# The second feed-forward product of a decoder layer by 26 products over 4 token, 4 feature and 2 column blocks, with input sums on GpSimd and products chained in PSUM

## The chip, the core and the metric

The kernel runs on one core of a Trainium2 chip. Time is the device time of one execution in microseconds; the number that counts is the median of the runs. The engines are named as in the profile: PE (TensorE, matmul), PEld (its weight loads), DVE (VectorE), ACT (ScalarE), POOL (GpSimd) and SP (SyncE, which issues most of the transfers).

## The reference

One layer for 2048 tokens of width 1024, in float32: a norm, a combined input projection, gated linear attention in four heads and dilated window attention in eight, an output projection, and then the part that the change touches:

```python
h = h + jnp.einsum('bsm,md->bsd', mixed, w_out[l])

nm = rmsnorm(h, mlp_norm_g[l])
a = jnp.square(jax.nn.relu(jnp.einsum('bsd,df->bsf', nm, w_ff1[l])))
h = h + jnp.einsum('bsf,fd->bsd', a, w_ff2[l])
return rmsnorm(h, final_norm_g)
```

`a` is 2048 x 4096, `w_ff2` is 4096 x 1024. `a` is called the activations below, and its product with `w_ff2` the second product.

## The kernel before

Every float32 operand of a matmul is split into a high part in `fp32r` (ScalarE, a copy that rounds) and a low part, the difference (VectorE; `split`, L346 and L347). `mm3` (L67 to L69) then makes three matmuls of each pair: high x high, low x high, high x low, all into one PSUM bank. The weights side of such a matmul is 128x128, the moving side 128x512.

Both feed-forward products are computed by a Strassen scheme over 2 x 2 x 2 blocks: seven block products in place of eight, in the order j = 1, 2, 5, 6, 3, 4, 7, with sums of blocks made ahead (inputs) and behind (outputs).

*First product.* Tokens stand in two halves. A group `g` is 256 features of one half; there are 16 groups in each, 32 in all, and a job is one of the seven products of a group, 12 matmuls. `prep1` splits the weights of the job that comes two later (with four sums on the weights, L1090 to L1095) and `product1` runs the job. Its results go through PSUM into four accumulators c11, c12, c21, c22 of 128x512, are squared after a ReLU (`square`, L1118 and L1119, on ScalarE), and become inputs of the second product's Strassen scheme: four sums of 128x512 on VectorE per group (L1144 to L1147), and seven stores into `actD` (L1122). GpSimd has nothing to do there. Between the halves the seven transformed inputs (`hb`) are loaded and split anew.

*Second product.* It runs over 14 phases, which are the seven products for each half. A phase has 8 steps of 2 blocks of 128 features and 4 tiles of 128 tokens, so 8 x 2 x 4 x 3 = 192 matmuls, into four PSUM banks. `prep_a` splits a step's activations (128x1024, `ca` from `ra`), `prep_b` the weights (`cb` from `rb`), with sums on VectorE (L1235) where the scheme wants them; `taken` adds a finished bank to the running sums of the output (L1276), and `output` applies the last norm, with a gain on GpSimd (L1252), and stores. The banks rotate over the four PSUM tags a, c, d and o, 8 banks in all.

A scheduler that simulates the engines sets the order of instructions on each engine from the order of the code; an engine then runs its instructions strictly in that order. Transfers are mostly issued on SP, also in order, so a transfer that waits for its data holds back those behind it. Large buffers are slots of one ring (`slot`, 25 of them), handed out in turn.

```python
def mm2(p, n, c, i):
    l, r = comb_a[n % 3], comb_b[n % 8]
    tk = slice(i * 128, i * 128 + 128)
    mm3(p, l[:, 0, c, tk], l[:, 1, c, tk], r[:, 0, c], r[:, 1, c], n % 8 == 0 and c == 0, n % 8 == 7 and c == 1)
```

Of the kernel before, what the change touches and what calls it, by code (L numbers as in the profile page):

```python
# [10 lines left out]
F32 = mybir.dt.float32  # L11
# [29 lines left out]

def emit(tc, a, stop=99):
# [23 lines left out]
    def mm3(out, sh, sl, mh, ml, first, last):  # L66
        T.matmul(out, sh, mh, start=first, stop=False)  # L67
        T.matmul(out, sl, mh, start=False, stop=False)  # L68
        T.matmul(out, sh, ml, start=False, stop=last)  # L69
# [10 lines left out]
    V.memset(mhalf, -0.5)  # L80
    stats = const.tile([128, 96], F32, name="stats")
# [61 lines left out]
    actD = dram.tile([7, 2, FF // 256, 128, 512], F32, name="actD")  # L143
    tD = dram.tile([2, FF // 256, 128, 512], F32, name="tD")
# [960 lines left out]
    def product1(at):  # L1105
        g, j = jobs1[at]
        half, gh = divmod(g, NP)
        if not acc1:
            acc = [slot("acc1") for _ in range(4)]
            acc1.extend(t[:, 512 * q:512 * q + 512] for t in acc for q in range(4))  # L1110
        X, c11, c12, c21, c22, s2, s4 = acc1[7 * (g % 2):7 * (g % 2) + 7]
# [9 lines left out]
        def store(q, n, v):  # L1121
            q.dma_start(actD[n - 1, half, gh], v)  # L1122

        if j in (1, 5, 4):
            A.activation({1: X, 5: c22, 4: c21}[j], p, AF.Copy)
        elif j == 2:
            V.tensor_tensor(c11, p, X, op=OP.add)
            square(c11)
            store(A, 1, c11)
# [3 lines left out]
        elif j == 3:  # L1133
            V.tensor_tensor(c12, p, c12, op=OP.add)
            square(c12)
        else:
            V.tensor_tensor(X, p, X, op=OP.add)
            V.tensor_tensor(c21, c21, X, op=OP.add)
            V.tensor_tensor(c22, c22, X, op=OP.add)
# [43 lines left out]
    w2 = a["w_ff2"].rearrange("o (c p) n -> p (o c) n", p=128)  # L1183
    out2 = a["out"].rearrange("o s d -> (o s) d")
    order2 = (1, 2, 5, 6, 3, 4, 7)
    phases = [(j, half) for j in order2 for half in range(2)]
    raw_a, comb_a, raw_b, comb_b, sums = [], [], [], [], {}

    def load_a(n):

        if n < 4 * len(phases):
            j, half = phases[n // 4]
            if len(raw_a) < 2:
                raw_a.append(view(slot("ra"), (4, 512)))
            SP.dma_start(raw_a[n % 2], actD[j - 1, half, 4 * (n % 4):4 * (n % 4) + 4].rearrange("c p s -> p c s"))

    def prep_a(n):

        if n >= 8 * len(phases):
            return
        if len(comb_a) < 3:
            comb_a.append(view(slot("ca", FR), (2, 2, 512)))
        c = comb_a[n % 3]
        split(c[:, 0], c[:, 1], raw_a[n // 2 % 2][:, n % 2 * 2:n % 2 * 2 + 2])
        if n % 2:
            load_a(n // 2 + 2)  # L1210

    def load_b(n):

        if n >= 56:
            return
        j, c = order2[n // 8], 2 * (n % 8)
        if len(raw_b) < 2:
            raw_b.append(view(slot("rb2"), (2, 2, 512)))
        pairs2 = tD.rearrange("k c p s -> k p c s")
        of = {(k, m): w2[:, 2 * c + k:2 * c + k + 3:2, 512 * m:512 * m + 512] for k in range(2) for m in range(2)}  # L1220
# [204 lines left out]
```

## Time and profile before

| what | us |
|---|---|
| median of 3 runs (2354.55 to 2360.78) | 2357.18 |
| span of the profiled execution | 2353.6 |
| TensorE busy in it | 2288.2 |
| VectorE busy | 1563.8 |
| ScalarE busy | 1148.4 |
| GpSimd busy | 516.7 |

The profiled execution's own total isn't listed apart from its span; the runs shown lie 1 to 7 us above that span. A group's row reads: line, engine, operation, output tile <- input tiles, shapes and count, then busy time in us and mean in ns, then the idle time of the engine just before these instructions and what ended it. A row of the timeline has start and duration in us first. A row of a stretch has its length, the busy time of PE, PEld, DVE, ACT and POOL with counts, the clock that TensorE was granted (1.00 is full), the share of the transfer engines and GB/s.

### The profile page before, as it was taken

To read this page: it belongs to the slowest core of one execution; us is meant where nothing else is said; L and a number is where in the kernel's file an instruction comes from. 1 tells how busy PE (TensorE), PEld (TensorE's weight loads), DVE (VectorE), ACT (ScalarE), POOL (GpSimd) and SP (SyncE) were. 2 spreads that over 40 slices of the span, in tenths; PEclk is the share of its full clock that TensorE was granted. 3 is DMA by queue.
4 is the path that set the end of the run, shared out by engine and by line. 5 is a ranking of instruction groups with operands and counts; after the bars stand their busy time and mean duration, and the time that the engine had idled before them with its cause. 6 is when DMAs were issued, how large, how long until landed. Compare 5 with 4: busy or idle time off the path is not lost.

```text
span 2353.6 us, 34983 instructions
## 1 busy us (share of the span) xinstructions
PE 2288.2 (97%) x12648; PEld 1976.9 (84%) x12648; DVE 1563.8 (66%) x2873; ACT 1148.4 (49%) x2202; POOL 516.7 (22%) x578
## 2 busy tenths in 40 slices
PE   5999999999999997999999999999999999999998
PEld 5977899789999996888888888888888888888886
DVE  6888767766667676345877779777764356446545
ACT  5575536534677673223655557555554223224323
POOL 4343224236468768000000000000000100001002
PEclk9999999999999998999999999999999999999999
DMA  6458743857577755567844447444476486457643
GB/s 158 122 161 251 236 155 110 263 168 249 182 228 238 251 183 185 183 215 254 263 154 148 148 148 273 148 152 154 158 264 236 169 284 239 146 178 249 212 165 108
DMA packets 340939, 458.11 MB, mean 195 GB/s; under 512 B 18020, under 2 KB 214133, under 8 KB 334494
## 3 DMA queue, kind: packets, MB, share of 16 engines
q1 hardware_dynamic: 336014, 447.23, 58.4%
q10 hardware_dynamic: 4752, 8.65, 1.0%
q8 instruction: 99, 1.62, 0.3%
q14 instruction: 74, 0.61, 0.1%
HBM read 293.51 MB, written 167.02 MB: 196 GB/s over the span
## 4 chain that ended last, share of the span: by engine, by line
PE 85%; DMA 5%; DVE 4%; issue 2%; POOL 2%; ACT 2%; SPq 0%; POOLq 0%; DVEq 0%; ACTq 0%
PE ps_a L68 9%; PE ps_a L69 9%; PE ps_a L67 9%; PE ps_c L69 7%; PE ps_c L68 7%; PE ps_c L67 7%; PE ps_d L67 4%; PE ps_d L69 4%; PE ps_d L68 4%; PE ps_a L684 4%; PE ps_o L67 3%; PE ps_o L68 3%; PE ps_o L69 3%; PE ps_d L665 2%; PE ps_c L643 2%
## 5 line engine op out<-in xcount | busy, mean ns | idle before, releaser
L1252 POOL TENSOR_TENSOR suma<-suma,gs 128x512 f32<-128x512 f32 x16 | 23.3, 1470 | 1142.2 <-ACT scr L1250 1142.1
L347 DVE TENSOR_TENSOR ca<-ra,ca 128x1024 fp32r<-128x1024 f32 x112 | 137.8, 1231 | 165.6 <-ACT ca L346 165.6
L346 ACT ACTIVATE ca<-ra 128x1024 fp32r<-128x1024 f32 x112 | 117.9, 1053 | 222.2 <-PE ps_c L69 183.5
L346 ACT ACTIVATE w1comb<-w1raw 128x512 fp32r<-128x512 f32 x224 | 140.1, 627 | 157.2 <-PE ps_c L69 58.9
L347 DVE TENSOR_TENSOR w1comb<-w1raw,w1comb 128x512 fp32r<-128x512 f32 x224 | 154.2, 691 | 55.1 <-ACT w1comb L346 55.1
L656 ACT ACTIVATE pe<-pe,O 128x256 f32<-128x256 f32 (+1 forms) x384 | 155.6, 454 | 52.0 <-DVE O L655 50.3
L684 PE MATMUL ps_a<-v,pt 128*128 128x65 f32 x1200 | 178.0, 251 | 2.3 <-ACT pt L672 2.0
L684 PEld LDWEIGHTS ps_a<-v,pt 128*128 128x128 f32 x1200 | 174.5, 193 | 4.3 <-ACT pt L672 2.4
L665 PE MATMUL ps_d<-ident,pe 128*128 128x128 f32 x600 | 158.6, 278 | 1.1 <-ACT pe L656 1.1
L655 DVE CUSTOM_DVE_ANT_0 pe<-ps_c,nb 128x256 f32<-128x256 f32 (+1 forms) x384 | 126.4, 361 | 37.8 <-PE ps_d L665 15.6
L202 ACT ACTIVATE wcomb<-wraw 128x512 fp32r<-128x512 f32 (+2 forms) x126 | 96.9, 773 | 86.9 <-POOL wraw L208 14.6
L346 ACT ACTIVATE cb<-rb 128x1024 fp32r<-128x1024 f32 x56 | 59.4, 1061 | 162.8 <-PE ps_o L68 111.4
L69 PE MATMUL ps_c<-hb,w1comb 128*128 128x512 f32 x336 | 130.9, 389 | 0.0
L67 PE MATMUL ps_c<-cb,ca 128*128 128x512 f32 x336 | 130.8, 389 | 0.0
L68 PE MATMUL ps_c<-cb,ca 128*128 128x512 f32 x336 | 130.8, 389 | 0.0
L68 PE MATMUL ps_c<-hb,w1comb 128*128 128x512 f32 x336 | 130.8, 389 | 0.0
L69 PE MATMUL ps_c<-cb,ca 128*128 128x512 f32 x336 | 130.8, 389 | 0.0
L67 PE MATMUL ps_c<-hb,w1comb 128*128 128x512 f32 x336 | 130.8, 389 | 0.0
L204 DVE TENSOR_TENSOR wcomb<-wraw,wcomb 128x512 fp32r<-128x512 f32 (+2 forms) x84 | 99.3, 1188 | 36.7 <-ACT wcomb L202 36.4
L665 PEld LDWEIGHTS ps_d<-ident,pe 128*128 128x128 f32 x600 | 108.3, 185 | 1.8 <-ACT pe L656 1.5
L347 DVE TENSOR_TENSOR cb<-rb,cb 128x1024 fp32r<-128x1024 f32 x56 | 68.3, 1222 | 61.9 <-ACT cb L346 61.9
L67 PE MATMUL ps_a<-wcomb,tb 128*128 128x256 f32 (+1 forms) x336 | 97.9, 292 | 9.3 <-ACT tb L346 3.7
(359 smaller groups left out, 7206.3 us busy)
## 6 DMA issues: line engine op xcount, KB each, us to landing
ra<-actD SPq DMA_DIRECT2D x56, 1024.0 KB, 6.3
actD<-acc SPq DMA_DIRECT2D x192, 256.0 KB, 2.5
rb<-w_ff SPq DMA_DIRECT2D x72, 512.0 KB, 4.6
w1raw<-w_ff SPq DMA_DIRECT2D x32, 1024.0 KB, 5.5
k<-kD SPq DMA_DIRECT2D x16, 1024.0 KB, 9.3
rb<-hTD SPq DMA_DIRECT2D x13, 1024.0 KB, 5.7
wraw<-w_in SPq DMA_DIRECT2D x48, 256.0 KB, 3.3
cmb<-boD SPq DMA_DIRECT2D x16, 528.0 KB, 6.0
```

Source lines behind the costliest of these rows:

```text
L67: T.matmul(out, sh, mh, start=first, stop=False)
L68: T.matmul(out, sl, mh, start=False, stop=False)
L69: T.matmul(out, sh, ml, start=False, stop=last)
L202: A.activation(hi, src, AF.Copy, scale=sc)
L204: V.tensor_tensor(lo, src, hi.bitcast(F32), op=OP.subtract)
L346: A.activation(hi, src, AF.Copy)
L347: V.tensor_tensor(lo, src, hi.bitcast(F32), op=OP.subtract)
L643: T.matmul(s, q, k_cols(k1, br, first), start=True, stop=False)
L655: V.tensor_tensor_reduce(p, s, bias, scale=1.0, scalar=BIG, op0=OP.add, op1=OP.min, accum_out=nm)
L656: A.activation(p, p, AF.Exp, bias=nm, scale=-1.0)
L665: T.transpose(pb[:, i * 128:i * 128 + 128], src, ident)
L684: T.matmul(self.b.opsum[:, n % 4], self.pt[:, i * 128:i * 128 + 128], self.b.v[:, blk, cols], start=first, stop=last)
```

## The change

The second product is made over 4 token blocks, 4 feature blocks and 2 column blocks at a time: 26 block products in place of the 32 of a plain product (the Strassen scheme before makes 28 of them). A table `PRODUCTS` says for each product which stored activation row it takes, whether it starts a new PSUM bank or goes on in the one of the product before it, its sign, and which outputs the bank is then added to; `WEIGHTS` says which weight blocks are loaded and summed, `SUMS` how the 26 activation rows come out of the 16 blocks of a pair of groups.

- In `product1` the four VectorE sums and the stores go. The four accumulators of a group now stand in one slot of four, and the intermediate X in two other places.
- `token_sums` makes, for each pair of groups, 28 sums of 128x256 on GpSimd, two or three behind each job of the next pair, and stores 26 rows of 128x256 (four of them are blocks without a sum).
- The second product has 52 phases (26 products x 2 halves) of 8 steps, each step one block of 128 features x 2 tiles of 128 tokens x 3 matmuls, into two banks. `prep_s` splits activations (two pieces of 128x1024 a phase), `prep_t` weights (four pieces of 128x1024 a weight, six buffers), `add_t` sums weights on GpSimd (128x1024), all at steps that are fixed ahead of their use.
- `taken` adds a bank to one to four outputs in the two steps after its phase. `output` squares each half row when it is finished.
- The ring has 26 slots.

```diff
-        return up.tile([128, SLOT], dt, name=name, tag="u", bufs=25)[:, :n]
+        return up.tile([128, SLOT], dt, name=name, tag="u", bufs=26)[:, :n]
...
-            square(c22)
-            square(c21)
-            store(SP, 4, c22)
-            store(SP, 2, c21)
-            V.tensor_tensor(X, c12, c22, op=OP.add)
-            V.tensor_tensor(s2, X, c11, op=OP.subtract)
-            V.tensor_tensor(c12, c11, c12, op=OP.subtract)
-            V.tensor_tensor(s4, c21, s2, op=OP.subtract)
-            for n, v in ((5, X), (6, s2), (7, c12), (3, s4)):
-                store(SP, n, v)
+            square(c21)
+            square(c22)
...
+        for l, r in SINGLES:
+            store(r, t[l])
+        yield
+        for l, x, op, y, r in SUMS:
+            G.tensor_tensor(t[l], t[x], t[y], op=OP.add if op == "+" else OP.subtract)
+            if r is not None:
+                store(r, t[l])
+            yield
...
+        for cs, x in parts:
+            A.activation(v[:, 0, cs], x, AF.Copy, scale=float(sign))
+            if sign == 1:
+                V.tensor_tensor(v[:, 1, cs], x, v[:, 0, cs].bitcast(F32), op=OP.subtract)
+            else:
+                V.scalar_tensor_tensor(v[:, 1, cs], x, -1.0, v[:, 0, cs].bitcast(F32), op0=OP.mult, op1=OP.subtract)
+        load_s(ph + 2, u)
...
+            G.tensor_tensor(d, x, y, op=OP.add if op == "+" else OP.subtract)
+            if stored:
+                SP.dma_start(tD[:, 2 * u:2 * u + 2], d)
...
+        for l, sign in PRODUCTS[k][3]:
+            m, n = divmod(l, 2)
+            c = sums[half, m][:, i, 512 * n:512 * n + 512]
+            V.tensor_tensor(c, c, p, op=OP.add if sign > 0 else OP.subtract)
+            if last_at[l] == k:
+                output(half, l, i)
...
+        mm3(p, l[:, 0, c % 4, tk], l[:, 1, c % 4, tk], r[:, 0, c % 2], r[:, 1, c % 2],
+            PRODUCTS[ph // 2][1] == 1 and c == 0, c == 7, PRODUCTS[ph // 2][1] == 0)
...
+    for ph in range(2 * NR):
+        for u, n in ((0, -7), (1, -3)):
+            at_step(4 if (ph, u) == (1, 1) else 8 * ph + n, prep_s, ph, u)
...
+        for u in range(4):
+            at_step(at + (-16, -12, -9, -6)[u], add_t, q, u)
+        for u in range(4):
+            at_step(at + ((-12, -8, -5, -2) if q else (-10, -8, -5, -2))[u], prep_t, q, u)
```

In the order of VectorE, the end of one group and the start of the next in the first product, before (`w1comb` is the split weights, `w1raw` the raw ones, `acc` the accumulators, `ps_` a PSUM bank):

```order
L1137 TENSOR_TENSOR acc_11516<-ps_d,acc_11516 128x512
L1093 TENSOR_TENSOR w1raw<-w1raw 128x4x128
L1138 TENSOR_TENSOR acc_11517<-acc_11517,acc_11516 128x512
L1139 TENSOR_TENSOR acc_11517<-acc_11517,acc_11516 128x512
L347 TENSOR_TENSOR w1comb<-w1raw,w1comb 128x512
L1095 TENSOR_TENSOR w1raw<-w1raw 128x4x128
L347 TENSOR_TENSOR w1comb<-w1raw,w1comb 128x512
L1127 TENSOR_TENSOR acc_11515<-ps_o,acc_11515 128x512
L1144 TENSOR_TENSOR acc_11516<-acc_11517 128x512
L347 TENSOR_TENSOR w1comb<-w1raw,w1comb 128x512
L1145 TENSOR_TENSOR acc_11518<-acc_11516,acc_11517 128x512
L1146 TENSOR_TENSOR acc_11517<-acc_11517 128x512
```

The same place after the change, where L1192 is the old L1127, the first drain of a group (`gs` and `xt` hold X):

```order
L1201 TENSOR_TENSOR xt<-ps_d,xt 128x512
L1161 TENSOR_TENSOR w1raw<-w1raw 128x4x128
L1202 TENSOR_TENSOR acc_11517<-acc_11517,xt 128x512
L1203 TENSOR_TENSOR acc_11517<-acc_11517,xt 128x512
L415 TENSOR_TENSOR w1comb<-w1raw,w1comb 128x512
L1163 TENSOR_TENSOR w1raw<-w1raw 128x4x128
L415 TENSOR_TENSOR w1comb<-w1raw,w1comb 128x512
L1192 TENSOR_TENSOR acc_11518<-ps_a,gs 128x512
L415 TENSOR_TENSOR w1comb<-w1raw,w1comb 128x512 x2
L1195 TENSOR_TENSOR gs<-ps_c,gs 128x512
L415 TENSOR_TENSOR w1comb<-w1raw,w1comb 128x512
L1196 TENSOR_TENSOR acc_11518<-gs,acc_11518 128x512
```

The sums L1144 to L1147 have gone from between the splits, and what is left stands in the order that it had.

On GpSimd, before, the last sums of the attention stand directly ahead of the small powers of the norms and the gains of the second product (L1252); nothing of the first product is between them:

```order
L742 TENSOR_TENSOR cmb<-cmb,small 128x4x128 x2
L744 TENSOR_TENSOR O_9490<-O_9490,cmb 128x4x128 x2
L94 TENSOR_TENSOR stats<-stats,mhalf 128x1 x16
L1252 TENSOR_TENSOR suma<-suma,gs 128x512 x5
L94 TENSOR_TENSOR stats<-stats,mhalf 128x1 x2
```

After the change the same place begins the sums of the first pair of groups (`xt` also holds the three extra tiles that sums are made in):

```order
L812 TENSOR_TENSOR O_9491<-O_9491,cmb 128x4x128 x2
L162 TENSOR_TENSOR stats<-stats,mhalf 128x1 x16
L1224 TENSOR_TENSOR xt<-acc_11517 128x256
L1224 TENSOR_TENSOR acc_11517<-acc_11517 128x256 x2
L1224 TENSOR_TENSOR xt<-acc_11517,acc_11518 128x256
L1224 TENSOR_TENSOR acc_11517<-acc_11518 128x256
L1224 TENSOR_TENSOR acc_11518<-acc_11518 128x256
```

These run in their fixed order through the 16 pairs, 448 in all, before the first weight sum (L1320) of the second product.

In the second product VectorE's order has, after the change, the additions of a bank (L1364) between the low parts of activations (L1298 and L1300, `cs` from `rs`) and of weights (`ct` from `rt`):

```order
L1364 TENSOR_TENSOR acc_11518<-acc_11518,ps_c 128x512
L1364 TENSOR_TENSOR acc_11518<-acc_11518,ps_o 128x512
L1298 TENSOR_TENSOR cs<-rs,cs 128x1024
L415 TENSOR_TENSOR ct<-rt,ct 128x1024 x2
L1298 TENSOR_TENSOR cs<-rs,cs 128x1024
L1364 TENSOR_TENSOR sum<-sum,ps_a 128x512
L1364 TENSOR_TENSOR sum<-sum,ps_c 128x512
L1300 SCALAR_TENSOR_TENSOR cs<-rs,cs 128x1024
```

Before, the sums of weights (L1235) stood among the low parts, and the additions came for four banks together:

```order
L347 TENSOR_TENSOR cb<-rb_15946,cb 128x1024
L347 TENSOR_TENSOR cb<-rb_15942,cb 128x1024
L347 TENSOR_TENSOR ca<-ra,ca 128x1024
L1235 TENSOR_TENSOR rb_15946<-rb_15946 128x1024
L1276 TENSOR_TENSOR sumb<-sumb,ps_a 128x512
L1276 TENSOR_TENSOR sumb<-sumb,ps_d 128x512
L1276 TENSOR_TENSOR sumb<-sumb,ps_c 128x512
L1235 TENSOR_TENSOR rb_15942<-rb_15942 128x1024
```

The weight sums have moved to GpSimd, and the additions to places between low parts, two banks at a time.

More of the change, by code (lines that the diff above doesn't have):

```diff
@@ L1108, in product1 @@
         if not acc1:
[L1109 to L1111 removed]
+            acc1.extend(slot("acc1") for _ in range(4))
+        X = gM[:, :512] if g % 2 else xt[:, :512]
+        c11, c12, c21, c22 = [acc1[g % 4][:, 512 * n:512 * n + 512] for n in range(4)]
         p = bank()
@@ L1181, in emit @@
         late = (h, u[:, 0], t)
-    w2 = a["w_ff2"].rearrange("o (c p) n -> p (o c) n", p=128)
+    w2 = a["w_ff2"].rearrange("o (c q p) n -> q p (o c) n", q=4, p=128)
     out2 = a["out"].rearrange("o s d -> (o s) d")
[L1185 to L1199, printed above, removed]
@@ L1308, in emit @@
+    for k, (m, at) in enumerate(first_at.items()):
+        for half in range(2):
+            at_step(16 * at + 8 * half - 1 if at else 2 * half * k + k - 7 + 7 * half, load_c, half, m)
+    for ph in range(2):
+        for u in range(2):
+            at_step(4 * ph + u - 20, load_s, ph, u)
     rb.append(slot("rb"))
@@ L1330, in emit @@
         product1(at)
+        for _ in range(2 if at % 14 else 3):
+            next(ts, None)
+        if at % 14 == 13:
+            ts = token_sums(at // 7)
         for n in parts_at.get(at, ()):
```

270 lines of the change are left out of this document (146 added, 124 removed), and 31 rows, old and new, of tables (SUMS, WEIGHTS).

## The prediction

> **What bounds the kernel now.** The page first (engines, then the chain), then the stretches of the span, and last the groups of the two feed-forward products.
>
> ```profile
> span 2353.6 us, 34983 instructions
> PE 2288.2 (97%) x12648; PEld 1976.9 (84%) x12648; DVE 1563.8 (66%) x2873; ACT 1148.4 (49%) x2202; POOL 516.7 (22%) x578
> PE 85%; DMA 5%; DVE 4%; issue 2%; POOL 2%; ACT 2%; SPq 0%; POOLq 0%; DVEq 0%; ACTq 0%
> ...
> 900.00:1000.00 100.00, 88.50 (x454) 74.04 (x453) 49.39 (x77) 24.59 (x56) 36.34 (x58) 0.93 0.48 156
> ...
> 1160.00:1400.00 240.00, 240.00 (x1061) 198.86 (x1060) 180.67 (x280) 134.17 (x230) 0.00 (x0) 1.00 0.44 150
> 1400.00:1460.00 60.00, 59.53 (x263) 48.98 (x262) 54.36 (x77) 43.18 (x68) 0.00 (x0) 1.00 0.73 257
> 1460.00:1730.00 270.00, 270.00 (x1193) 223.72 (x1192) 205.50 (x318) 154.15 (x261) 0.00 (x0) 1.00 0.47 161
> 1740.00:2340.00 600.00, 599.60 (x2646) 496.42 (x2645) 306.07 (x329) 197.02 (x241) 28.74 (x26) 1.00 0.59 204
> ```
>
> The columns of a stretch are its length, busy time of PE, PEld, DVE, ACT and POOL, then clock, DMA share and GB/s. From 1160 us on TensorE has no gap and its clock is full: in the first product (to about 1737 us) it loses 0.47 us, where the second half's inputs are reloaded, and in the second product 0.40 us. Only fewer matmuls help here, and nothing else is late yet. 599.6 us / 2646 = **0.2267 us a matmul**; the means of 389 and 390 ns below overlap and aren't the pitch.
>
> ```profile
> L67 PE MATMUL ps_c<-cb,ca 128*128 128x512 f32 x336 | 130.8, 389 | 0.0
> L69 PE MATMUL ps_o<-cb,ca 128*128 128x512 f32 x112 | 43.6, 390 | 0.0
> ```
>
> These are the first and last of twelve such groups (four PSUM tags, three lines): 1008 + 672 + 672 + 336 = 2688 matmuls, as 14 phases x 8 x 2 x 4 x 3 say.
>
> **Term 1, the matmuls.** 26 products x 2 halves x 8 blocks x 2 token tiles x 3 = 2496 of the same form and order (128x128 against 128x512, three into one bank). 192 fewer x 0.2267 = **-43.5 us**, all on the path.
>
> **Term 2, the end.** After the last matmul the old code makes two sums and two squares before the norm; the new one makes one of each, since the other half row was squared before.
>
> ```profile
> 2344.85 0.69 DVE L1276 TENSOR_TENSOR suma<-suma,ps_o 128x512 f32<-128x512 f32 x1
> 2346.05 0.61 ACT L1250 ACTIVATE scr<-suma 128x512 f32<-128x512 f32 x1
> 2346.89 0.63 ACT L1250 ACTIVATE scr<-sumd 128x512 f32<-128x512 f32 x1
> ```
>
> The one square can start at about 2345.6 instead of 2346.89: **-1.3 us**. Its cover, the earlier sum and square of the other half row, is products away.
>
> **Term 3, the first product.** Per group of 256 features the four sums on VectorE (L1144 to L1147) go, 8 per pair of groups; GpSimd gets 28 sums of 128x256 per pair. A pair is 168 matmuls x 0.2267 = 38.1 us. Rows for one sum:
>
> ```profile
> L813 POOL TENSOR_TENSOR gla<-gla 128x256 f32<-128x256 f32 x16 | 11.7, 730 | 0.2
> L261 POOL TENSOR_TENSOR acc<-acc,misc 128x248 f32<-128x248 f32 x16 | 17.5, 1098 | 22.8 <-DVE acc L260 16.4 <-issue 6.4
> 100.00:200.00 100.00, 95.09 (x520) 78.10 (x521) 86.50 (x151) 67.74 (x153) 36.42 (x34) 1.00 0.53 161
> actD<-acc SPq DMA_DIRECT2D x192, 256.0 KB, 2.5
> ```
>
> Alone it takes 0.73 us; a slightly smaller one took 1.10 in stretches like this one, with VectorE 86.5% busy. Two of the 28 overwrite a tile whose store has just been issued (the second sum after the first, the seventh after the fifth); with 2.5 us a store I put 5 us for both. GpSimd then needs 28 x 0.73 + 5 = 25.4 to 28 x 1.10 + 5 = 35.8 us of 38.1: it fits, and four accumulators let it run into the next pair.
>
> What it costs VectorE is a port:
>
> ```profile
> 230.24 0.68 DVE L304 TENSOR_TENSOR acc<-ps_c,acc 128x512 f32<-128x512 f32 x1
> 230.47 1.29 POOL L214 TENSOR_TENSOR wraw<-wraw 128x512 f32<-128x512 f32 x1 [1.90 <-DVE wcomb L206]
> 230.84 1.47 DVE L206 SCALAR_TENSOR_TENSOR wcomb<-wraw,wcomb 128x512 fp32r<-128x512 f32 x1
> ...
> 297.89 1.22 DVE L204 TENSOR_TENSOR wcomb<-wraw,wcomb 128x1024 fp32r<-128x1024 f32 x1
> 299.03 1.22 DVE L347 TENSOR_TENSOR tb<-xp,tb 128x1024 fp32r<-128x1024 f32 x1
> ...
> 298.51 4.01 POOL L208 TENSOR_TENSOR wraw<-wraw 128x1024 f32<-128x1024 f32 x1 [18.85 <-DMA wraw<-w_in]
> 319.02 2.40 POOL L212 TENSOR_TENSOR wraw<-wraw 128x1024 f32<-128x1024 f32 x1
> ```
>
> L206, with both inputs in SBUF, takes 1.47 us and ends 0.55 after the GpSimd sum does; L304, with one input in PSUM, is not touched. The other way round the GpSimd sum at 298.51 takes 4.01 us where one of its size takes 2.40: two VectorE instructions, started every 1.14 us, kept it out. So they exclude each other, and VectorE's trains win. The Trainium skill states this exclusion (SBUF — State Buffer, § Who interferes with whom): whichever issues second blocks fully. By that rule, with the port held for whole instructions, the sum would be the second rival's 2341 and not 2317; the trace agrees that they exclude, but the 0.55 us behind the release shows less than the whole 0.69 held.
>
> ```profile
> 1457.73 0.68 DVE L1138 TENSOR_TENSOR acc<-acc 128x512 f32<-128x512 f32 x1
> 1458.33 0.68 DVE L1139 TENSOR_TENSOR acc<-acc,acc 128x512 f32<-128x512 f32 x1
> L347 DVE TENSOR_TENSOR w1comb<-w1raw,w1comb 128x512 fp32r<-128x512 f32 x224 | 154.2, 691 | 55.1 <-ACT w1comb L346 55.1
> ```
>
> Back to back a 128x512 costs VectorE 0.60 us (1457.73 to 1458.33), not 0.69. Left per pair are 36 (28 with two SBUF inputs, 8 from PSUM): 36 x 0.60 = 21.6 us; if each of the 28 waited for a whole sum (0.60 of it after overlap) 38.4 us, just the pair's 38.1. Operands are prepared two jobs (5.4 us) ahead, so steadily I cost nothing. What queues behind a blocked VectorE instruction is the drains and the low parts, and TensorE waits for both. The cover is thin from 1400 to 1460 us. There VectorE worked 54.4 of 60 us; 8 x 0.69 x 60/38.1 = 8.7 go and at most 28 x 0.60 x 60/38.1 = 26.5 come: 72.2, over by 12. I take a third, since trains win: **+4 us**. Bounds for the stage: 0, and 28 (second rival).
>
> **Term 4, the second product.** Per product TensorE works 96 x 0.2267 = 21.8 us. Rows for the rest:
>
> ```profile
> L347 DVE TENSOR_TENSOR ca<-ra,ca 128x1024 fp32r<-128x1024 f32 x109 | 134.1, 1231 | 165.6 <-ACT ca L346 165.6
> L346 ACT ACTIVATE ca<-ra 128x1024 fp32r<-128x1024 f32 x109 | 114.7, 1053 | 222.2 <-PE ps_c L69 183.5 <-PE ps_o L69 23.8 <-DMA ra<-actD 7.4
> L1276 DVE TENSOR_TENSOR suma<-suma,ps_c 128x512 f32<-128x512 f32 x12 | 8.2, 684 | 0.0
> L212 POOL TENSOR_TENSOR wraw<-wraw 128x1024 f32<-128x1024 f32 x4 | 10.5, 2619 | 0.2
> 1760.00:1770.00 10.00, 10.00 (x46) 8.27 (x45) 1.23 (x1) 1.06 (x1) 0.00 (x0) 1.00 1.05 391
> ```
>
> VectorE: 8 low parts x 1.23 + 38 additions x 4 / 26 = 5.8 x 0.68 = 13.8 us; ScalarE 8 x 1.05 = 8.4; GpSimd, in 18 of 24 weights, 4 sums x 2.6 = 10.5. All are under 21.8, and low parts are due 9 to 16 us after their place in the order. A drained bank is wanted again one phase (10.9 us) later, against some 43 before: a chained product continues in the bank that VectorE reads, so a late drain stops TensorE sooner. Transfers: 52 loads of 1 MB, 16 of 2 MB, 2 MB of kept sums, 8 in and 8 out, some 104 MB in 566 us = 184 GB/s, under the 204 of now. About the change of stages some 14 MB (6 of h, 4 of weights, 4 of inputs) are wanted in 45 us, 311 GB/s; the trace moved 391. I take **+1 us**; bounds 0 and 31 (third rival).
>
> **Term 5, the rest.** The 26th slot lets the scheduler start a few loads of the attention earlier. TensorE's idle 3.1 us there are the bound both ways; I take 0.
>
> ```profile
> 400.00:500.00 100.00, 96.88 (x414) 74.65 (x413) 76.25 (x112) 51.80 (x106) 33.36 (x26) 1.00 0.74 229
> ```
>
> **Sum.** 2353.6 - 43.5 - 1.3 + 4 + 1 = 2313.8 us of span. The median of the runs shown, 2357.18, is 3.6 above the profiled span; with that 2317.4, say **2317 us**.
>
> **The rivals.** *First, on the other side: the chain of sums outlasts its pair.* If every sum waits for a VectorE instruction in front of it (0.69 + 0.73 = 1.42 us), GpSimd needs 28 x 1.42 + 5 = 44.8 us a pair, and the first drain of a later pair (L1192) waits for its last stores: 6.7 x 15 = 100 us, so 2417. From (38.1 + 44.8/15 - 5) / 28 = 1.29 us a sum on, the whole gain of 44.8 is gone. For it: the 4.01 above. Against it: L261's 1.10 beside a VectorE that was busier than the 57% (21.6 of 38.1) left here.
>
> *Second: the port sets the pace.* If each side held it for its whole instruction, a pair takes 28 x 0.69 + 28 x 0.73 = 39.8 us: 1.7 x 15 = 26 us more, 28 with the change of halves, in place of my 4: 2341. Against it: the 0.55 us behind the release and the pitch of 0.60.
>
> *Third: the change doesn't deliver in its own stage.* If each GpSimd sum of 2.4 us stops a low part, VectorE needs 13.8 + 4 x 2.4 = 23.4 us a product, 1.6 over, in 18 products 29 us, with drains that come too late 31: 2347, about no change. Against it: VectorE's starts are 1.14, not 1.23 apart, and only four of its eight could be hit.
>
> **How the numbers follow.** Forecast 0.65 (2308 to 2330), second rival 0.17, third 0.08, first 0.10. The range reaches from 2308 (terms 3 and 4 at nothing, 5 at its best, and 1 less) to 2342, which takes the second rival's 2341 in and leaves out the first, the third and a worse second. About 0.3% or 7.1 us is what a measurement can tell from no change: faster (under 2350.1) 0.65 + 0.17 and a quarter of the third, 0.84; within 0.06; slower 0.10.
>
> **What would show it.** Term 1: 2496 matmuls at 0.227 us in the last stage, TensorE over 99% busy. Term 3: GpSimd's sums at 0.8 to 1.1 us, the last store of a pair landed before L1192 wants it, TensorE's gaps few and near the change of halves. Wrong if TensorE has a gap in every pair with L1192 waiting for a DMA (first), for a low part (second), or in every product of the last stage for VectorE (third), or if the granted clock falls below 1.00.

## The result and the profile after

| what | before | after |
|---|---|---|
| median (us) | 2358.35, 4 runs | 2439.34, 4 runs (2437.08 to 2440.94) |
| span of the profiled execution | 2353.6 | 2435.3 |

The change makes the kernel slower: 1.0343 times the time before, interval 1.0329 to 1.0358. The forecast was 2317 us; the time lies far above the range. In the changed kernel L1143 loads raw weights of the first product, L1158 to L1163 sum them, L414 and L415 make high and low parts, L1218 stores the rows of `token_sums`, L1224 is its sum, L1320 that of `add_t`, and L1109 loads the second half's inputs.

The page of the kernel after, with the lines that answer to those of before, and four of its groups (busy, mean ns of one | idle time before and what ended it):

```profile
span 2435.3 us, 35693 instructions
PE 2292.4 (94%) x12456; PEld 1964.1 (81%) x12456; DVE 1704.7 (70%) x2802; ACT 1166.5 (48%) x2227; POOL 1179.3 (48%) x1098
...
L415 DVE TENSOR_TENSOR w1comb<-w1raw,w1comb 128x512 fp32r<-128x512 f32 x224 | 186.9, 838 | 65.3 <-ACT w1comb L414 65.1
L414 ACT ACTIVATE w1comb<-w1raw 128x512 fp32r<-128x512 f32 x224 | 135.5, 624 | 200.8 <-DVE w1raw L1160 179.3
...
L1224 POOL TENSOR_TENSOR acc<-acc,acc 128x256 f32<-128x256 f32 x128 | 139.5, 1094 | 2.4
L1158 DVE TENSOR_TENSOR w1raw<-w1raw 128x512 f32<-128x512 f32 x32 | 22.4, 701 | 159.1 <-DMA w1raw<-w_ff 159.1
```

TensorE has 192 matmuls fewer, as the change says, and is still busy for 4 us more. GpSimd's 1179 us are not the news: its sums take 1.01 us on average in the first product, inside the prediction's 0.73 to 1.10. The news is the last row: VectorE stands 159 us before the first sum on a new group's weights, because their load has not landed. Next the stretches of after, with the columns of the prediction:

```profile
1160.00:1400.00 240.00, 218.01 (x914) 177.00 (x913) 148.69 (x194) 108.69 (x193) 133.72 (x140) 0.95 0.39 123
1400.00:1460.00 60.00, 55.86 (x245) 45.55 (x244) 39.15 (x51) 28.51 (x51) 38.63 (x40) 1.00 0.41 130
1460.00:1730.00 270.00, 241.41 (x1000) 193.72 (x999) 182.91 (x229) 132.37 (x229) 168.47 (x167) 0.96 0.48 152
1740.00:1840.00 100.00, 91.00 (x384) 73.47 (x383) 68.57 (x83) 48.09 (x82) 65.04 (x63) 0.97 0.43 129
1840.00:1960.00 120.00, 105.68 (x430) 84.84 (x429) 83.77 (x72) 36.34 (x38) 64.29 (x41) 0.93 0.74 255
1960.00:2330.00 370.00, 370.00 (x1634) 306.68 (x1633) 290.21 (x239) 143.00 (x156) 158.82 (x60) 1.00 0.47 159
```

The first product, without a gap before, now loses 7 to 11% of each stretch in idleness, and its clock is below 1.00 in most of them. VectorE is less busy than before (148.7 of 240 against 180.7), so it is no bound. The second product loses at its start (430 matmuls in 120 us, where 0.2267 us each would give 529) and has no gap from 1960 to 2330 us. Behind that it loses once more: from 2330 to 2350 us it starts 70 matmuls where 88 would fit, the larger of two gaps being

```profile
2344.96 0.50 PE L135 MATMUL ps_a<-ct,cs 128*128 128x512 f32 x1 [2.02 <-DVE cs L1300]
```

Here it waits for a low part of activations, while VectorE is busy without a break from 2340 to 2350 us beside GpSimd's weight sums.

By the timelines, in spans: the first product begins 4.0 us later (1127.55 against 1123.55); it takes 708.0 instead of 614.5 us (to the end of its last matmul's 0.2267 us), **+93.6**; the second takes 592.5 instead of 606.6, where 43.5 less were due, **+29.4**; what follows the last matmul is 1.7 us shorter. 4.0 + 93.6 + 29.4 - 43.5 - 1.7 = 81.8, but for rounding the difference of the spans, 81.7. (Before, 15 matmuls of the second product stand ahead of the first's last one, after only 4; with these counted where they belong, the losses are 96.1 and 27.0.)

The waits in the first product, for VectorE, TensorE and SP's queue (waiting engine and line, what ended it: us in all, times, longest):

```profile
DVE w1raw L1158 <- DMA w1raw<-w_ff: 155.0, 28, 9.8
PE ps_a L135 <- DVE w1comb L415: 27.5, 9, 4.7
PE ps_c L135 <- DVE w1comb L415: 16.3, 8, 4.6
...
SPq L1218 <- POOL xt L1224: 169.8, 102, 7.0
SPq L1218 <- ACT acc L1187: 156.4, 32, 11.0
SPq L1218 <- POOL acc L1224: 154.9, 203, 2.4
```

and VectorE's wait for the same load before:

```profile
DVE w1raw L1090 <- DMA w1raw<-w_ff: 27.0, 30, 2.4
```

TensorE waits for low parts, they for sums of weights, those for the load; and SP, which issues that load, spends 325 us waiting for GpSimd's sums, so as to issue their stores, and 156 us for ScalarE's squares, which the four rows without a sum need. Each pair has two such loads; most of the 155 us fall on the second, which stands behind the sums' last stores. Parts of one pair, from the timeline of after (start and duration first; SP, GpSimd, VectorE, then TensorE):

```profile
1248.63 0.32 SPq L1218 DMA_DIRECT2D actD<-xt  x1
1249.45 0.32 SPq L1218 DMA_DIRECT2D actD<-acc  x1
1249.86 0.67 SPq L1143 DMA_DIRECT2D w1raw<-w_ff  x1
...
1218.83 0.74 POOL L1224 TENSOR_TENSOR xt<-acc,acc 128x256 f32<-128x256 f32 x1 [13.85 <-ACT acc L1187]
...
1248.68 1.43 POOL L1224 TENSOR_TENSOR acc<-acc 128x256 f32<-128x256 f32 x2
1264.32 0.74 POOL L1224 TENSOR_TENSOR xt<-acc,acc 128x256 f32<-128x256 f32 x1 [14.20 <-ACT acc L1187]
...
1308.92 0.74 POOL L1224 TENSOR_TENSOR xt<-acc,acc 128x256 f32<-128x256 f32 x1 [13.92 <-ACT acc L1187]
...
1257.11 0.69 DVE L1158 TENSOR_TENSOR w1raw<-w1raw 128x512 f32<-128x512 f32 x1 [9.80 <-DMA w1raw<-w_ff]
...
1253.36 0.39 PE L134 MATMUL ps_a<-hb,w1comb 128*128 128x512 f32 x1
1258.46 0.80 PE L135 MATMUL ps_a<-hb,w1comb 128*128 128x512 f32 x1 [4.71 <-DVE w1comb L415]
1259.05 0.63 PE L136 MATMUL ps_a<-hb,w1comb 128*128 128x512 f32 x1
1259.48 0.63 PE L134 MATMUL ps_a<-hb,w1comb 128*128 128x512 f32 x1
...
1262.89 0.61 PE L136 MATMUL ps_a<-hb,w1comb 128*128 128x512 f32 x1
1263.32 0.42 PE L134 MATMUL ps_d<-hb,w1comb 128*128 128x512 f32 x1
1263.57 0.40 PE L135 MATMUL ps_d<-hb,w1comb 128*128 128x512 f32 x1
```

The load goes out 0.09 us after the store that stands before it on SP, and that store had waited for nearly the last sums of the pair, at 1249.4. It lands 7.25 us later; VectorE had been idle for 9.80. Meanwhile GpSimd, through at 1250.1, idles for 14.20 us: the next pair's sums need blocks that come out of the stalled products. That is a loop: this pair's sums had begun at 1218.8, so 31.0 us of sums until the load is issued + 7.3 of load + 7.2 until the next sums can begin = 45.5 us, and the next pair, to 1308.9, takes 44.6, where TensorE's work is 38.1. 15 pairs of that kind would lose 98 to 111 us; 93.6 were lost.

TensorE pays for the gap twice. After 4.71 us of idleness it starts matmuls 0.427 us apart, not 0.227, ten times in a row: 2.0 us more. In the stretch 1160 to 1400 us it is idle for 22.0 us, and its 914 matmuls took 218.0 instead of 914 x 0.2267 = 207.2: a third of the loss is slow clock.

### The profile page after: what moved, and what is told of

Read it like the earlier page. It is cut to its first block, busy times and chain, and to the rows that moved or that the text cites. A ratio compares the mean times of both kernels' runs of the same rounds, so it can differ in the third digit from the quotient of the medians.

```text
span 2435.3 us, 35693 instructions
## 1 busy us (share of the span) xinstructions
PE 2292.4 (94%) x12456; PEld 1964.1 (81%) x12456; DVE 1704.7 (70%) x2802; ACT 1166.5 (48%) x2227; POOL 1179.3 (48%) x1098
## 5 line engine op out<-in xcount | busy, mean ns | idle before, releaser
L415 DVE TENSOR_TENSOR w1comb<-w1raw,w1comb 128x512 fp32r<-128x512 f32 x224 | 186.9, 838 | 65.3 <-ACT w1comb L414 65.1
L414 ACT ACTIVATE w1comb<-w1raw 128x512 fp32r<-128x512 f32 x224 | 135.5, 624 | 200.8 <-DVE w1raw L1160 179.3
L1296 ACT ACTIVATE cs<-rs 128x1024 fp32r<-128x1024 f32 x104 | 109.2, 1051 | 190.1 <-PE ps_c L136 92.9
L1224 POOL TENSOR_TENSOR xt<-acc,acc 128x256 f32<-128x256 f32 x48 | 45.0, 937 | 259.9 <-ACT acc L1187 207.7
L162 POOL TENSOR_TENSOR stats<-stats,mhalf 128x1 f32<-128x1 f32 (+1 forms) x64 | 46.1, 723 | 247.4 <-DVE stats L161 247.3
L415 DVE TENSOR_TENSOR ct<-rt,ct 128x1024 fp32r<-128x1024 f32 x68 | 121.6, 1794 | 41.2 <-ACT ct L414 41.1
L1186 ACT ACTIVATE acc<-acc 128x512 f32<-128x512 f32 x128 | 80.4, 631 | 142.7 <-DVE acc L1198 59.7
L136 PE MATMUL ps_c<-ct,cs 128*128 128x512 f32 x360 | 141.9, 394 | 0.0
L134 PE MATMUL ps_c<-ct,cs 128*128 128x512 f32 x360 | 141.8, 394 | 0.0
L135 PE MATMUL ps_c<-ct,cs 128*128 128x512 f32 x360 | 141.6, 393 | 0.0
L1224 POOL TENSOR_TENSOR acc<-acc,acc 128x256 f32<-128x256 f32 x128 | 139.5, 1094 | 2.4
L1158 DVE TENSOR_TENSOR w1raw<-w1raw 128x512 f32<-128x512 f32 x32 | 22.4, 701 | 159.1 <-DMA w1raw<-w_ff 159.1
L1224 POOL TENSOR_TENSOR acc<-acc 128x256 f32<-128x256 f32 x128 | 128.1, 1006 | 3.8
```

Source lines behind the costliest of these rows:

```text
L134: T.matmul(out, sh, mh, start=first, stop=False, skip_group_check=more)
L135: T.matmul(out, sl, mh, start=False, stop=False, skip_group_check=more)
L136: T.matmul(out, sh, ml, start=False, stop=last, skip_group_check=more)
L414: A.activation(hi, src, AF.Copy)
L415: V.tensor_tensor(lo, src, hi.bitcast(F32), op=OP.subtract)
L1224: G.tensor_tensor(t[l], t[x], t[y], op=OP.add if op == "+" else OP.subtract)
```

## The experiments

Two theories were set against each other. **Q, the queue**: loads stand on SP behind stores that wait for GpSimd's chain of sums. **P, the port**: GpSimd's sums stretch VectorE's instructions, and low parts come late. All are edits of the changed kernel; times are medians, and ratios are to the kernel before, which took 2358.2 to 2358.9 us beside them from the fifth kernel on.

**1. The raw weights' loads on another queue.**

```diff
-            SP.dma_start(raw1[g % 2], w1[:, :, g0:g0 + 256])
+            A.dma_start(raw1[g % 2], w1[:, :, g0:g0 + 256])
```

> The loads of raw first-product weights (w1raw) are issued on ScalarE's queue instead of SP's; nothing else is edited. Theory Q (in the changed kernel these loads stand on SP behind stores that wait for GpSimd's sums, come about 7 us late once a pair, and TensorE then also runs slowly for some us): the waits of L1158 for w1raw, 159 us in all, go, the first product falls from about 705 us to 610 to 620, the total to 2345 to 2360. Theory P (the port: GpSimd's sums slow VectorE's low parts, 0.69 to 0.84 us): the stall stays where it is, total 2425 to 2445.

Measured: 2372.48 us, ratio 1.0070 (1.0048 to 1.0092). One word is worth 66.9 us, though the time is 12 us above Q's range. In the profiled execution the first product falls from 708.0 to 635.6 us, and the second stays (593.9 against 592.5). Its stretches, and VectorE's wait there:

```profile
1160.00:1400.00 240.00, 240.00 (x1060) 198.73 (x1059) 172.85 (x223) 127.71 (x225) 157.92 (x168) 1.00 0.45 139
1400.00:1500.00 100.00, 90.58 (x372) 72.25 (x371) 80.95 (x97) 55.96 (x92) 61.74 (x55) 0.95 0.62 199
```

```profile
DVE w1raw L1158 <- DMA w1raw<-w_ff: 52.0, 31, 2.7
```

All sums are still made, beside a VectorE that is busier than in the changed kernel, and TensorE has no gap from 1160 to 1400. So it was the queue there. What is left lies mostly at the change of halves (from 1400) and in the second product.

**2. The token sums left out.**

```diff
-            G.tensor_tensor(t[l], t[x], t[y], op=OP.add if op == "+" else OP.subtract)
             if r is not None:
-                store(r, t[l])
+                store(r, t[l % 16])
```

> The 448 sums of activations on GpSimd are left out (each store takes an unsummed block, so the output isn't the reference's); stores, loads and queues stay. Q and P alike: the first product at 610 us, since no store waits and no port is shared. It prices the sums as a whole: total 2320 to 2345. If it stays above 2400, the cause lies in neither, but in the stores or loads themselves.

Measured: 2324.02 us (two runs), ratio 0.9857 (0.9838 to 0.9877), 7 us above the forecast; without its sums the kernel no longer computes the layer, but loads, stores and matmuls are in place. The first product takes 615.1 us (614.5 before), the second 572.1, where its 2492 matmuls behind the first's last one are worth 564.9. The sums with their consequences cost 115 us.

**3. Sums made, stores that don't wait for them.**

```diff
-                store(r, t[l])
+                store(r, gF[:, :256])
```

> GpSimd makes all sums, but the stores of summed rows take a constant tile, so that no store waits for a sum and no sum for a store (the output isn't the reference's). Q: SP flows, first product at 610 to 615 us, total 2325 to 2350, though the port is shared as before. P: the low parts stay at 0.84 us and the first product above 680 us, total above 2410.

Measured: 2418.01 us (two runs), in P's range, but the total misleads. With nothing to wait for, the scheduler issued these stores much earlier, in the stage of the output projection, where TensorE waited 56 us for loads; the first product begins at 1215.7 us instead of 1127.5. From there on the kernel shows what was wanted (the first product runs to 1834.2 us, its change of halves lies near 1530):

```profile
1400.00:1500.00 100.00, 100.00 (x443) 82.77 (x442) 76.83 (x96) 54.65 (x94) 69.36 (x72) 1.00 0.25 79
1500.00:1740.00 240.00, 234.76 (x1028) 192.18 (x1027) 196.41 (x235) 138.06 (x233) 178.77 (x173) 1.00 0.31 99
1740.00:1850.00 110.00, 110.00 (x487) 91.10 (x486) 84.39 (x97) 62.47 (x102) 79.69 (x78) 1.00 0.36 127
```

GpSimd makes all its sums (69 of 100 us from 1400 on), and TensorE stops only for 5.2 us at the change of halves, for low parts. The first product takes 618.5 us: 4.0 more than before, 3.4 more than without sums. So the sums, with the port that they share, cost the first product 3 to 4 us when no store waits for them; the rest of its loss hangs on the stores and what they wait for. The comparison has one blemish: the early stores also left fewer transfers to this stage, 79 to 127 GB/s against 123 to 152 in the changed kernel.

**4. The weight sums of the second product on VectorE.**

```diff
-            G.tensor_tensor(d, x, y, op=OP.add if op == "+" else OP.subtract)
+            V.tensor_tensor(d, x, y, op=OP.add if op == "+" else OP.subtract)
```

> The 72 weight sums of the second product are made by VectorE instead of GpSimd. Q: the first product isn't touched; in the last stage the waits stem from loads held on SP, so the total falls by 0 to 8 us, 2431 to 2440. P: low parts fall from 1.8 to 1.23 us and the last stage loses its 26 us over TensorE's 566: total 2413 to 2420.

Measured: 2425.4 us, 13.9 us less than the changed kernel, between the two theories. In the profiled executions the second product falls from 592.5 to 580.0 us and the first does not gain (710.2). It is won at two places: 466 matmuls instead of 430 from 1840 to 1960 us, 8 us' worth, and 90 instead of 70 from 2330 to 2350, 4.5 us' worth. A weight sum and a low part in the groups of the changed kernel:

```profile
L1320 POOL TENSOR_TENSOR rt<-rt 128x1024 f32<-128x1024 f32 x24 | 68.9, 2889 | 82.3 <-DMA rt<-w_ff 74.0 <-DVE ct L415 8.2
L415 DVE TENSOR_TENSOR ct<-rt,ct 128x1024 fp32r<-128x1024 f32 x68 | 121.6, 1794 | 41.2 <-ACT ct L414 41.1
```

and with the sums on VectorE:

```profile
L1320 DVE TENSOR_TENSOR rt<-rt 128x1024 f32<-128x1024 f32 x24 | 28.6, 1221 | 14.8 <-DMA rt<-w_ff 14.8
L415 DVE TENSOR_TENSOR ct<-rt,ct 128x1024 fp32r<-128x1024 f32 x58 | 71.8, 1246 | 27.3 <-ACT ct L414 27.0
```

Apart, the two operations take 1.22 and 1.25 us on one engine; together, on two engines, 2.89 and 1.79. The slower engine takes longer for its sum alone than VectorE for both operations.

**5. The token sums on VectorE.**

```diff
-            G.tensor_tensor(t[l], t[x], t[y], op=OP.add if op == "+" else OP.subtract)
+            V.tensor_tensor(t[l], t[x], t[y], op=OP.add if op == "+" else OP.subtract)
```

> The 448 token sums run on VectorE instead of GpSimd; stores and loads keep their queue. Queue theory (a raw weight load stands on SP behind stores that wait for the chain of sums): the chain is shorter (28 sums of about 0.35 us by the 0.60 us of a 128x512, against 1.02 on GpSimd), so the 159 us that VectorE waits for w1raw fall below 60, and the time to 2340 to 2385. Port theory (VectorE and GpSimd exclude each other, and that stretches the first product): the first product is whole, 1125 to 1740 has under 5 us of TensorE idle, and the time is 2325 to 2345. Rival to both: VectorE, in order, now waits itself for the two stores that must land before their tile is overwritten (some 5 us a pair), drains come late, and it stays over 2400.

Measured: 2375.8 us, ratio 1.0072 (1.0057 to 1.0088). VectorE's wait for raw weights falls from 159 to 76.5 us, not below 60, but the time is in Q's range. P's range is missed, and the first product is not whole (660.3 us). That alone does not refute P, since VectorE now has the sums to make as well.

**6. All loads off SP.** As 1, and on ScalarE's queue also the second half's inputs (L1109), the kept activations (L1282), the raw weights of the second product (L1312) and the starting values (L1336).

> All loads that can stand behind a store of sums go to ScalarE's queue: raw weights of both products, the second half's inputs, the kept activations, the sums' starting values. Stores stay on SP. Queue theory: of the 48 us that the first of these kernels (raw weights of the first product on ScalarE's queue, 2372.5) lies above the one without sums (2324.0), the change of halves (13 us) and most of the change of stages (24 us) go: 2330 to 2350. Port theory: what is left there is the port, so 2367 to 2378. Rival: ScalarE, in order, waits at these issues for the buffers, its squares and high parts come late, and it is slower than 2378.

Measured: 2363.3 us, ratio 1.0013 (0.9999 to 1.0026): 9.2 less than 1, outside both ranges, 13 above Q's. ScalarE, in order, now waits at these issues: before its high parts in the second product it stood 17.5 us in two waits for stores of activations to land.

**7. Edits 1 and 4 together.**

> The raw weight loads of the first product on ScalarE's queue, and the weight sums of the second product on VectorE. Queue theory: the weight sums matter only near the change of stages, so 2360 to 2372 against 2372.5. Port theory: the 14 us that the weight sums on VectorE brought alone come again in full or more: 2340 to 2359.

Measured: 2359.17 us, ratio 1.0005. 13.3 less than 1, as edit 4 brought alone, and just between the two ranges: the two add, and Q alone is not the whole story.

**8. Edits 1, 4 and 5 together.**

> All sums of the change on VectorE and the raw weight loads of the first product on ScalarE's queue; GpSimd does next to nothing in either product. Queue theory: stores no longer lag, nothing waits behind them: 2325 to 2345, TensorE idle under 10 us from 1125 to 1740. Port theory: the same or better, 2318 to 2335. Rival (VectorE becomes the bound: in the first product some 36 x 0.60 + 28 x 0.35 = 31 of 38 us a pair, in the second 13.8 + 18/24 x 4 x 1.2 = 17.4 of 21.8 us a product, with waits for stores and loads in its order): 2350 to 2400.

Measured: 2373.77 us, ratio 1.0061. Both theories missed, and the time is in the rival's range. That VectorE becomes the bound fits it, but VectorE also still waited 79.5 us for raw weights, so the run does not separate the two. The first product takes 665.0 us, no less than in 5 (660.3): with the sums on VectorE, the queue of that load is not what holds it.

**9. The stores on GpSimd's own queue.** 10 adds edit 4, and 11 is edit 5 with these stores.

```diff
-            SP.dma_start(actD[r, half, :, c], v)
+            G.dma_start(actD[r, half, :, c], v)
```

> The stores of the sums are issued from GpSimd's own queue, behind the sums that they store; SP carries loads only, and no load stands behind a sum any more, nor a store behind a load. Nothing else differs from the changed kernel. Queue theory: the whole loss in the first product, at the change of halves and at the change of stages goes at once: VectorE's waits for w1raw under 55 us, 2328 to 2350. Port theory: 2370 to 2400. Rival: what GpSimd pays to issue a store is unknown here; if it is 0.4 us or more, 28 sums of 1.02 and 24 issues exceed the pair's 38.1 us, and the time is above 2400.

> As the run before it, and the weight sums of the second product on VectorE. Queue theory: the 13 us that this brought twice (2439.3 to 2425.4, 2372.5 to 2359.2) are smaller here, since the stores no longer wait behind loads: 2322 to 2340. Port theory: 13 us less than the run before, whatever that is.

> The token sums on VectorE, their stores from GpSimd's queue, which waits for VectorE and does nothing else meanwhile in the first product. Queue theory: against 2375.8 with the stores on SP, the loads come in time and what is left is VectorE's own load and its waits for stores: 2335 to 2360. If VectorE's load alone were the reason for those 2375.8, it stays within 6 us of them.

Measured: 2521.65, 2511.04 and 2366.06 us; edit 4 brings 10.6 us here. The groups of 9 from 1100 to 1900 us show the price that was unknown:

```profile
L1218 POOL DMA_DIRECT2D actD<-acc x271 | 149.4, 552 | 171.8 <-ACT acc L1187 165.3 <-POOL acc L1224 5.7
```

A store costs GpSimd 0.55 us, 14 us for the 26 of a pair, which with some 24 us of sums is about TensorE's 38.1 us before any wait. The four stores of a pair that wait for ScalarE's squares now stand in its chain too, 165 us in all; in the changed kernel its sums themselves waited 226 us for squares. The rival held. Kernel 11 gains 9.7 us over 5, half-way between its two answers.

**12. The second half's inputs on GpSimd's queue**, on top of 7.

```diff
-        SP.dma_start(t[:, :2048], hTD[half, j - 1].rearrange("p c s -> p (c s)"))
+        (G if half else SP).dma_start(t[:, :2048], hTD[half, j - 1].rearrange("p c s -> p (c s)"))
```

> On top of the kernel with the first product's raw weights on ScalarE's queue and the weight sums on VectorE (2359.2): the loads of the second half's inputs, which there waited on SP behind stores of sums (the high parts of the inputs waited 8.9 us for such a load), go to GpSimd's queue. Queue theory: the change of halves loses little any more (1400 to 1500 us: TensorE busy over 95 instead of 89 us), 2343 to 2353. Port theory (what is lost there is VectorE's load and the exclusion): 2356 to 2362. Rival: on GpSimd's queue the loads stand behind the sums themselves, just as before: no change either, with the high parts still waiting for the load.

Measured: 2366.93 us, 7.8 more than 7. From 1400 to 1500 us ScalarE's longest wait for such a load is now 13.0 us:

```profile
ACT hb L414 <- DMA rb<-hTD: 16.1, 3, 13.0
```

The rival's mechanism held: behind the sums themselves the loads stand no better than behind their stores. That it would change nothing did not hold; the time is above all three answers.

**13. Edits 6 and 4 together.**

> All loads on ScalarE's queue (2363.3 alone) and the weight sums on VectorE (13 to 14 us twice). Queue theory: the two add, 2346 to 2354. If both mend the same place, 2355 to 2363.

Measured: **2350.26 us, ratio 0.9960 (0.9944 to 0.9975)**, faster than both kernels, if only by 0.4% than the one before. 8.9 us less than 7, as 6 was 9.2 less than 1: the remedies add, as Q had it.

**14 and 15. The change of stages**, on top of 12: the first raw weights and the starting values of the second product on ScalarE's queue; and with that the last pair's sums on VectorE.

> On top of the first kernel of this batch: the first raw weights and the starting values of the second product are loaded from ScalarE's queue, so that at the change of stages, too, SP has nothing but the stores and the loads of kept activations. Queue theory: of the 15 us lost from 1740 to 1850 at least 8 go: 2334 to 2346. Port theory: within 4 us of the first kernel of this batch.

> As the kernel before it, and the sums of the last pair of groups (28 of 448) on VectorE, so that the activations that the second product reads first are stored sooner. Queue theory: 2328 to 2342, faster than before. Rival: VectorE, in order, waits for the two stores inside the chain and the drains come late: no gain over the kernel before it, or up to 10 us more.

Measured: 2366.19 and 2357.99 us. So moving these loads does not free the second product's start; taking the last pair's chain off GpSimd does, for 8 us. In the profiled executions the second product takes 584.4 and 570.2 us; the first gives part of it back (642.0 and 647.6).

**16 and 17. The sums kept away from the change of halves**, on top of 13: four sums behind a product before and after it, none in it; 17 has the last pair's sums on VectorE as well.

```diff
-        for _ in range(2 if at % 14 else 3):
+        for _ in range(4 if 98 <= at < 106 or 118 <= at < 126 else 0 if 106 <= at < 118 else 2 if at % 14 else 3):
```

> On top of the kernel with all loads on ScalarE's queue and the weight sums on VectorE (2350.3): no token sum is issued in the twelve products in which the second half's inputs are split (VectorE has no gap there from 1420 to 1447 us, and its low parts of 128x1024 take 1.75 instead of 1.22 us beside the sums); the sums go before and behind them, four to a product. Port theory for this stage: TensorE is busy over 94 of the 100 us from 1400 on instead of 89.7, and the time is 2340 to 2347. Queue theory, with nothing left behind stores: within 3 us of 2350. Rival: the denser sums before and behind stretch VectorE there and give the gain back.

> The same, and the last pair's 28 sums on VectorE, which brought 8 us where loads stood on SP. With the loads already on ScalarE's queue the last pair matters less: 2 to 6 us under the kernel before it. Rival: nothing, or some us more, since VectorE's drains come late there.

Measured: 2350.6 and 2350.5 us. Inconclusive: GpSimd worked through that stretch all the same (28.2 us of 40 from 1420 to 1460, 24.1 without the edit). What 15 brought is not there a second time.

**18. That one pair's sums left out**, on top of 13.

```diff
-            G.tensor_tensor(t[l], t[x], t[y], op=OP.add if op == "+" else OP.subtract)
+            if g != 13: G.tensor_tensor(t[l], t[x], t[y], op=OP.add if op == "+" else OP.subtract)
             if r is not None:
-                store(r, t[l])
+                store(r, t[l if g != 13 else l % 16])
```

> On top of the kernel with all loads on ScalarE's queue and the weight sums on VectorE (2350.3): the 28 sums of the one pair of groups whose sums run while the second half's inputs are split are left out; its stores stay and take the tiles as they are. Port theory for this place: TensorE is busy over 37 of the 40 us from 1420 to 1460 (30.5 there), the low parts of 128x1024 take 1.2 instead of 1.4 us, and the time is 2338 to 2344. Queue theory, with stores that stand before nothing: the loss is the loads' own, and the time stays within 3 us of 2350.

Measured: 2344.8 us, ratio 0.9952 (0.9939 to 0.9966), 5.5 less than 13 and 0.8 above the range of P. That difference is not clear of the noise: the runs of 13 lie from 2345.1 to 2350.8, those of 18 from 2343.0 to 2349.3, and the two intervals overlap. The same 40 us in kernel 13,

```profile
1420.00:1460.00 40.00, 30.54 (x130) 23.50 (x128) 34.79 (x37) 23.65 (x36) 24.10 (x21) 1.00 0.66 221
```

and without these sums:

```profile
1420.00:1460.00 40.00, 36.87 (x155) 29.79 (x154) 37.14 (x47) 31.44 (x49) 9.51 (x8) 0.96 0.60 197
```

In these two executions TensorE is idle for 6.3 us less there. The port is not shown to be the whole of it. Kernel 13's waits from 1410 to 1470 us are

```profile
PE ps_c L134 <- ACT w1comb L414: 5.5, 2, 3.3
PE ps_d L135 <- DVE w1comb L415: 3.4, 2, 2.6
ACT w1comb L414 <- DMA actD<-acc: 4.1, 1, 4.1
PE ps_c L135 <- DVE w1comb L415: 1.5, 1, 1.5
```

Half of TensorE's idleness, 4.9 us, is for low parts, the side that the port can stretch. The other half, 5.5 us, is for high parts from ScalarE, which had itself stood 4.1 us for a store. And the edit takes away more than the port: these stores no longer wait for sums either. Kernel 3, with its sums made at this place, lost 5.2 us there.

## Why the prediction was wrong

**The ladder.** 2439.3, less 66.9 for the raw weights' loads (1), less 13.3 for the weight sums (edit 4, in 7), less 8.9 for the other loads (13): 2350.3. The next 5.5 us, for one pair of sums at the change of halves (18), are not clear of the noise. The remaining 20.8 us down to the kernel without sums (2324.0) lie, by the profiled executions, mostly in the first product (632.4 us in 18 against 615.1) and less in the second (576.3 against 572.1); they were not taken apart further. That kernel kept its loads on SP and its weight sums on GpSimd, so it is no bound for 13.

**Terms 1, 2 and 5 held**, or nearly. 1634 matmuls in 370 us are 0.2264 us each; the end is 1.7 us shorter, 1.3 was said; the first product starts 4.0 us later, where 3.1 was the bound. That start is not firm: in the kernels above, whose edits lie behind it, it falls between 1121.9 and 1133.0 us (kernel 3 apart), so steps of a few us between them are not to be read as one cause.

**Term 3 failed, +4 against +93.6**, at "Operands are prepared two jobs (5.4 us) ahead, so steadily I cost nothing". The lead of prepared operands covers a late low part. It does not cover the raw weights, whose load is issued by SP in order, and the change had put 22 stores a pair on that queue which wait for GpSimd's chain. The prediction counted GpSimd's work (25.4 to 35.8 us of 38.1; it was 31.3 in the pair shown, 1218.8 to 1250.1) and concluded that it fits. It does fit; but work that fits in a period may still be too late inside it, and what stood behind its stores was never listed. The prediction asked this of L1192, for its last stores, and not of the next row on SP, L1143. The second thing it missed is the slowed clock: a gap of 4.7 us costs 6.7. What the prediction did price, the port, came out at its size: 3 to 4 us in kernel 3 against its +4, and at the change of halves, where it had called the cover thin. That it took just a third of its bound for this was a guess.

**Term 4 failed too, +1 against +29.4** (27.0 by matmuls), near its bound of 31, and in two parts. *The change of stages*, some 22 us up to 1960 us, is the larger. The last pair's sums wait there for the store of a tile that they are to overwrite, made by 1845.0 us; SP issues it 19 us later, among loads:

```profile
1864.19 0.32 SPq L1218 DMA_DIRECT2D actD<-xt  x1
1873.12 0.74 POOL L1224 TENSOR_TENSOR xt<-acc 128x256 f32<-128x256 f32 x1 [26.46 <-DMA actD<-xt]
```

By kernel 15, taking this chain off GpSimd brings 14 us of the second product (584.4 to 570.2); how each gap of TensorE hangs on it was not followed. The transfer engines were also full from 1840 to 1870 us (share 1.01 to 1.03); in kernel 15 they were full from 1770 to 1790 (1.03 and 1.04), and TensorE had no gap there. *The weight sums on GpSimd* cost 12.5 us of the 27 by kernel 4: 8 of them at the change of stages, the other 4.5 the late low parts from 2330 to 2350 us. That is the third rival's mechanism, with low parts of 1.79 us and sums of 2.89 instead of 2.4. But it stops TensorE at these places only, and not in every product, as the rival had it.

**The rivals.** The first had the right side and nearly the size (2417, with the forecast's own 4 us still in it), but not the mechanism, so the closeness is luck. It decides from 1.29 us a sum, and the sums took 1.01 on average; no L1192 waited for a store. A loop through the load, not GpSimd's throughput, set the pace. The second, the port, would have cost 26 us in a steady first product; it cost 3 to 4. Chances of 0.84 for faster rested on engines' work alone; none of the cases had SP's order in it.

## What to carry to other kernels

When a change moves work to a slower engine, write down for each of its stores what the issuing queue holds behind it, and compare the time at which the last of these stores can go with the time at which the next load is wanted; that the work fits its period says nothing on this. Give loads that feed the bound engine a queue without waiting stores, and expect an engine's queue to bring that engine's own waits with it. A gap at TensorE is to be priced at more than its length.

## What was not expected of the hardware

**The clock after a gap.** In the changed kernel's two products every one of the 13 gaps of TensorE of 3.77 us or more was followed by 5 to 11 matmuls started 0.427 us apart, 1.1 to 2.3 us in all, sometimes only after a few at full pace. Below that it varied: gaps of 2.33 and 3.46 us were followed by none, those of 2.02, 2.62 and 2.85 by seven or eight. The Trainium skill (TensorE: Matmul & The Clock Gate, Part 1 on the clock gate) gives 426.7 ns from start to start for this width at half clock, and a window of idleness of some 3.4 us after which the clock falls. The trace agrees with the first, and with the second for the gaps of 3.77 us and more; but the clock also fell after gaps of 2.02 to 2.85 us, and did not after one of 3.46. The granted clock of a whole run, 0.976, hides it; the stretches show it.

**GpSimd as an issuer.** A store costs it 0.55 us, against 0.32 on SP, and during that time it makes no sums.

**Two engines slower than one.** With inputs in SBUF on both sides, a 128x1024 sum on GpSimd (2.89 us) and a low part on VectorE (1.79) take longer side by side than one after the other on VectorE (1.22 and 1.25). GpSimd's share of that is its own: alone, such a sum took it 2.40 to 2.62 us in the kernel before.
